# Attention output of a hybrid attention and RWKV-7 block: split values stationary, split exponentials moving, sums on GpSimd

## Chip, core and metric

The kernel runs on one core of one Trainium2 chip. The metric is device microseconds of one execution, lower is better; the median of three runs of the kernel before is 4223.68 us.

## What is computed

One layer of a diffusion block over 2048 latent tokens of width 1024 with a context prefix of 256 tokens. The part that the change touches is the banded attention: each of the 8 query heads (64 wide, 4 heads to a key and value head) reads the keys at most 128 tokens away, all 256 context keys and one sink, in one softmax.

```python
def latent_window_attention(q, k, v, kc, vc, sink):
    ...
    s_loc = jnp.einsum('bnqgrd,bnkgd->bngrqk', qb, kb).astype(jnp.float32) * scale
    s_ctx = jnp.einsum('bnqgrd,bcgd->bngrqc', qb, kc).astype(jnp.float32) * scale
    ...
    s_loc = jnp.where(valid[None, :, None, None], s_loc, -jnp.inf)
    ...
    p = jax.nn.softmax(jnp.concatenate([s_loc, s_ctx, s_sink], axis=-1), axis=-1)
    ...
    o = (jnp.einsum('bngrqk,bnkgd->bnqgrd', p_loc, vb)
         + jnp.einsum('bngrqc,bcgd->bnqgrd', p_ctx, vc))
    return o.reshape(B, L, N_Q_HEADS * dh)

def trunk_layer(x, xc, c, c_ctx, ...):
    ...
    ya = latent_window_attention(q, k, v, kc, vc, sink)
    ... # yr: bidirectional RWKV-7 scan, 64 wide heads, from the context's final state
    x = x + gate1 * merge_branches(ya, yr, gl, w_branch_attn, w_branch_rwkv, w_out)
    x = x + gate2 * sq_relu_mlp(modulate(rmsnorm(x, norm2_g), shift2, scale2), w_mlp_up, w_mlp_down)
```

## The kernel before

It runs in four stages. Until about 1100 us it normalises, projects and prepares the RWKV operands (`project`, `prepare`). From about 1100 to 2400 us the RWKV recurrence runs in 36 steps of 64 tokens and both directions, with the attention and a filler of gate and branch matrix products beside it. Then come merge and output projection, and from about 2750 us the MLP. The change lies in the second stage, apart from the line in `project` that stores the values.

**The recurrence.** A step goes through `chain_g` (TensorE, then a ScalarE copy of `g`), `chain_u` (TensorE, then ScalarE copies into `w`), `chain_s` (TensorE, then VectorE's product with `pc`), `turn` and `before` for the next step (TensorE into `gb`, then VectorE into `kr` and `bm`). Every four steps `inverse` inverts 32 by 32 triangles on VectorE: 31 pairs of small operations on `itmp` and `tn` (lines 588 and 590, each with two inputs in SBUF) and block transposes (lines 582, 599, 603).

**The attention.** There are 16 blocks of 128 queries. `scores(n)` loads the queries and (every second block) the keys, multiplies them head by head into `sc`, lets VectorE take minima of the rows, and writes the maximum as extra rows into `qB`. `outputs(n-1)` runs beside it: for each of 2 key heads `g` and each of 4 or 5 key blocks `b` (156 pairs in all) TensorE makes the transposed scores `sT`, 128 keys by 4 heads times 128 queries; ScalarE takes the exponential into `pT` (two buffers); and for each of the 4 heads a float32 product with `pT` as the stationary and `vtok` as the moving operand adds to `ops`. `vtok` holds 64 value columns and a column of ones, so column 64 of `ops` is the sum of the exponentials. VectorE adds the sink's term, takes the reciprocal and scales; TensorE transposes the result (`ot`), ScalarE copies it out, and it goes to `ya_d`.

**Order.** `attend` alternates steps of `scores` and `outputs`; `beside` runs one round of it, and one step of the filler `fill`, in every one of the six parts of a recurrence step. From this program order a scheduler sets each engine's order, and all engines run in order. `sc`, `sT`, `mt` and `ot` share two PSUM banks (`atp`), `ops` has one. All transfers go through SyncE's queue. A product of two operands that are split into two float32r parts is written as three float32r products (`gemm`, line 234).

## Time and profile before

| | us |
|---|---|
| runs (three), lowest, median, highest | 4222.08, 4223.68, 4229.45 |
| profiled execution | 4228.56 |
| its span, first to last instruction | 4226.8 |
| busy in the span: TensorE | 3865.3 (91%) |
| VectorE, ScalarE, GpSimd | 2171.9 (51%), 1359.5 (32%), 1349.6 (32%) |

Shares over the whole span mix stages with different limits: of GpSimd's 1349.6 busy us only 106.0 lie between 1130 and 2400 us, where the attention runs. So that stretch, from the first recurrence step to the last, is read by itself.

### The profile page before, as it was taken

To read this page: it belongs to the slowest core of one execution; us is meant where nothing else is said; L and a number is where in the kernel's file an instruction comes from. 1 tells how busy PE (TensorE), PEld (TensorE's weight loads), DVE (VectorE), ACT (ScalarE), POOL (GpSimd) and SP (SyncE) were. 2 spreads that over 40 slices of the span, in tenths; PEclk is the share of its full clock that TensorE was granted. 3 is DMA by queue.
4 is the path that set the end of the run, shared out by engine and by line. 5 is a ranking of instruction groups with operands and counts; after the bars stand their busy time and mean duration, and the time that the engine had idled before them with its cause. 6 is when DMAs were issued, how large, how long until landed. Compare 5 with 4: busy or idle time off the path is not lost.

```text
span 4226.8 us, 67796 instructions
## 1 busy us (share of the span) xinstructions
PE 3865.3 (91%) x26788; PEld 3148.4 (74%) x26788; DVE 2171.9 (51%) x3794; ACT 1359.5 (32%) x2476; POOL 1349.6 (32%) x1104
## 2 busy tenths in 40 slices
...
GB/s 236 202 195 158 161 183 188 188 185 184 164 138 138 125 131 148 106 132 96 131 139 83 158 150 179 176 154 65 70 50 40 60 41 130 69 60 60 40 55 45
DMA packets 617587, 529.95 MB, mean 125 GB/s; under 512 B 156212, under 2 KB 536340, under 8 KB 616244
## 3 DMA queue, kind: packets, MB, share of 16 engines
...
HBM read 381.09 MB, written 144.38 MB: 124 GB/s over the span
## 4 chain that ended last, share of the span: by engine, by line
PE 58%; DVE 6%; DMA 4%; issue 2%; POOL 2%; SPq 1%; ACT 1%; POOLq 0%; DVEq 0%; ACTq 0%
PE fd L1343 5%; PE fd L1344 5%; PE fd L1345 5%; PE fu L235 5%; PE fu L236 5%; PE fu L237 5%; PE ch L535 5%; PE gt L947 3%; PE ops L883 3%; PE gb L535 2%; DVE au L582 1%; PE sc L835 1%; PE mm L1260 1%; PE mm L1258 1%; PE mm L1259 1%
## 5 line engine op out<-in xcount | busy, mean ns | idle before, releaser
L235 PE MATMUL acc<-hh,w_hi 128*128 128x384 f32 (+6 forms) x1304 | 457.4, 353 | 41.6 <-ACT hh L211 18.9
L237 PE MATMUL acc<-hh,w_lo 128*128 128x384 f32 (+6 forms) x1304 | 455.8, 351 | 10.3 <-POOL w_lo L229 10.3
L236 PE MATMUL acc<-hl,w_hi 128*128 128x384 f32 (+6 forms) x1304 | 456.5, 351 | 4.8 <-POOL hl L212 4.8
L1349 DVE TENSOR_TENSOR acc<-fd,acc 128x512 f32<-128x512 f32 x480 | 322.3, 686 | 249.1 <-PE fd L1345 246.8
L235 PE MATMUL fu<-h2h,up_h 128*128 128x512 f32 x1024 | 403.4, 394 | 5.8 <-ACT rl L1330 5.8
L1343 PE MATMUL fd<-dn_h,g_h 128*128 128x512 f32 x1024 | 399.8, 390 | 3.5 <-DVE acc L1347 3.5
L236 PE MATMUL fu<-h2l,up_h 128*128 128x512 f32 x1024 | 402.6, 393 | 0.0
L237 PE MATMUL fu<-h2h,up_l 128*128 128x512 f32 x1024 | 402.0, 393 | 0.0
L1333 DVE TENSOR_TENSOR g_l<-rl,g_h 128x512 fp32r<-128x512 f32 x128 | 150.0, 1173 | 487.4 <-POOL rl L1332 487.4
L1344 PE MATMUL fd<-dn_l,g_h 128*128 128x512 f32 x1024 | 399.7, 390 | 0.0
L1345 PE MATMUL fd<-dn_h,g_l 128*128 128x512 f32 x1024 | 398.3, 390 | 0.0
L235 PEld LDWEIGHTS acc<-hh,w_hi 128*128 128x128 f32 (+2 forms) x1304 | 256.1, 197 | 67.1 <-ACT hh L211 21.8
L1332 POOL TENSOR_TENSOR rl<-rl 128x512 f32<-128x512 f32 x128 | 149.9, 1171 | 469.2 <-ACT g_h L1331 469.1
L229 POOL TENSOR_TENSOR w_lo<-w_raw,w_hi 128x1024 fp32r<-128x1024 f32 (+1 forms) x92 | 232.7, 2532 | 205.9 <-ACT w_hi L228 185.7
L1330 ACT ACTIVATE rl<-fu 128x512 f32<-128x512 f32 x128 | 76.2, 597 | 654.1 <-PE fu L237 644.9
L237 PEld LDWEIGHTS acc<-hh,w_lo 128*128 128x128 f32 (+2 forms) x1304 | 255.7, 196 | 31.4 <-POOL w_lo L229 12.5
L236 PEld LDWEIGHTS acc<-hl,w_hi 128*128 128x128 f32 (+2 forms) x1304 | 256.0, 196 | 25.1 <-POOL hl L212 6.0
L1287 POOL TENSOR_TENSOR dn_l<-raw,dn_h 128x1024 fp32r<-128x1024 f32 x64 | 155.6, 2450 | 275.1 <-ACT dn_h L1286 275.1
L845 DVE TENSOR_REDUCE mm<-sc 128x1 f32<-128x256 f32 (+1 forms) x256 | 119.0, 477 | 237.9 <-PE sc L837 152.2
L235 PEld LDWEIGHTS fu<-h2h,up_h 128*128 128x128 f32 x1024 | 193.1, 189 | 49.3 <-ACT rl L1330 6.0
L1343 PEld LDWEIGHTS fd<-dn_h,g_h 128*128 128x128 f32 x1024 | 192.9, 188 | 44.9 <-DVE acc L1347 4.0
L237 PEld LDWEIGHTS fu<-h2h,up_l 128*128 128x128 f32 x1024 | 192.7, 188 | 43.5
...
## 6 DMA issues: line engine op xcount, KB each, us to landing
...
```

The source lines that it names most:

```text
L229: pool.tensor_tensor(out=lo[:, :, :m], in0=raw[:, :, :m], in1=hi[:, :, :m].bitcast(F32), op=ALU.subtract)
L235: pe.matmul(ps[:m, :n], wh[:, k, :m], hh[:, k, :], start=(k == 0), stop=False)
L236: pe.matmul(ps[:m, :n], wh[:, k, :m], hl[:, k, :], start=False, stop=False)
L237: pe.matmul(ps[:m, :n], wl[:, k, :m], hh[:, k, :], start=False, stop=(k == KC - 1))
L535: return self.link(nc.tensor.matmul(*a, **k))
L1287: eng.tensor_tensor(out=lo, in0=raw, in1=hi.bitcast(F32), op=ALU.subtract)
L1332: pool.tensor_tensor(out=rl, in0=rl, in1=rl, op=ALU.mult)
L1333: dve.tensor_tensor(out=glo[:, j], in0=rl, in1=gh[:, j].bitcast(F32), op=ALU.subtract)
L1343: pe.matmul(ps, lh, dn[j][0][:, cs], start=(j == 0), stop=False)
L1344: pe.matmul(ps, lh, dn[j][1][:, cs], start=False, stop=False)
L1345: pe.matmul(ps, ll, dn[j][0][:, cs], start=False, stop=(j == FG - 1))
L1349: dve.tensor_tensor(out=acc[:, cs], in0=ps, in1=acc[:, cs], op=ALU.add)
```

## The change

The values are no longer kept in SBUF. `project` copies each transposed value tile once and stores it in `va_d`; `load_v` fetches a block of 128 tokens when the attention first needs it and splits it into a float32r part and a remainder, for head `g` side by side in 128 columns (in swapped order for the other head). In `outputs` the exponentials `pf` are split the same way: ScalarE copies them to `ph`, GpSimd subtracts into `pl`. Two float32r products, with the split values stationary and 512 moving columns (4 heads times 128 queries), replace the four float32 products; the output is then already transposed, with the two parts of the values in the two halves of the partitions, and VectorE adds the halves after a ScalarE copy. GpSimd adds the exponentials over the key blocks into `ts`; VectorE adds the sink's term into 8 partitions of `ts`; a float32 product with a matrix of ones sums over the partitions and broadcasts (`bc`), and VectorE takes the reciprocal of 128 by 512 elements and multiplies. `pT`, `ph` and `pl` have one buffer each. Keys are loaded for every block (384 tokens) rather than every second one (512), through the buffer `qraw` that queries and modulation weights use too.

```diff
@@ project
-                    for j in range(2):
-                        act.activation(vtok[:, t0 // P:t0 // P + n // P, j, 0:C],
-                                       tp[:, :n].rearrange("p (a b) -> p a b", b=P)[:, :, j * C:(j + 1) * C], AF.Copy)
+                    vt = epool.tile([P, 512], F32, name="st", bufs=3)
+                    act.activation(vt[:, :n], tp[:, :n], AF.Copy)
+                    sp.dma_start(out=va_d[t0 // P:(t0 + n) // P].rearrange("a p c -> p a c"),
+                                 in_=vt[:, :n].rearrange("p (a c) -> p a c", c=P))
...
+    def load_v(b):
+
+        raw = ap_.tile([P, 2, C], F32, name="vraw", bufs=1)
+        sp.dma_start(out=raw.rearrange("p g c -> p (g c)"), in_=va_d[b])
+        v = ap_.tile([P, 2, 2, C], F32R, name=f"vc{b}" if b < CTX // P else "vl", bufs=1 if b < CTX // P else 3)
+        for g in range(2):
+
+            act.activation(v[:, g, g], raw[:, g], AF.Copy)
+            dve.tensor_tensor(out=v[:, g, 1 - g], in0=raw[:, g], in1=v[:, g, g].bitcast(F32), op=ALU.subtract)
+        return v
...
+        raw = ap_.tile([P, 2, 512], F32, name="kraw", tag="qraw", bufs=1)
         for g in range(2):
-            raw = ap_.tile([P, 512], F32, name="kraw", tag="pT", bufs=2)
...
+        if n + 1 < NB:
+            load_kl(n + 1)
...
@@ outputs
-                pT = ap_.tile([P, NP, P], F32, name="pT", bufs=2)
-                act.activation(pT, sT, AF.Exp, scale=-1.0)
+                pf = ap_.tile([P, NP, P], F32, name="pT", bufs=1)
+                act.activation(pf, sT, AF.Exp, scale=-1.0)
+                ph = ap_.tile([P, NP, P], F32R, name="ph", bufs=1)
+                act.activation(ph, pf, AF.Copy)
+                pl = ap_.tile([P, NP, P], F32R, name="pl", bufs=1)
+                if b == 0:
+                    pool.tensor_copy(ts, pf)
+                else:
+                    pool.tensor_tensor(out=ts, in0=ts, in1=pf, op=ALU.add)
+                pool.tensor_tensor(out=pl, in0=pf, in1=ph.bitcast(F32), op=ALU.subtract)
                 yield
-                for a in range(NP):
-                    pe.matmul(op[:, a], pT[:, a], vtok[:, vb, g], start=(b == 0 and a == 0), stop=(b == nblk - 1),
-                              skip_group_check=True)
+                vg = v[:, g].rearrange("p a c -> p (a c)")
+                pe.matmul(op, vg, ph, start=(b == 0), stop=False)
+                pe.matmul(op, vg, pl, start=False, stop=(b == nblk - 1))
                 if b < nblk - 1:
                     yield
-            den = ap_.tile([P, 2, NP], F32, name="den", bufs=2)
-            dve.tensor_tensor(out=den[:, 0], in0=op[:, :, C], in1=k.es[:, g * NP:(g + 1) * NP], op=ALU.add)
-            dve.reciprocal(out=den[:, 1], in_=den[:, 0])
-            dve.tensor_tensor(out=on[:, :, g], in0=op[:, :, 0:C], in1=den[:, 1].unsqueeze(2).broadcast_to([P, NP, C]),
-                              op=ALU.mult)
+
+            r = hh[g]
+            act.activation(ob[r], op[hh[1 - g]].rearrange("p (a q) -> p a q", a=NP), AF.Copy)
+            dve.tensor_tensor(out=ob[r], in0=op[r].rearrange("p (a q) -> p a q", a=NP), in1=ob[r], op=ALU.add)
+            dve.scalar_tensor_tensor(out=ts[0:H], in0=k.tmp[0:H], scalar=cc[0:H, C_KS + g:C_KS + g + 1], in1=ts[0:H],
+                                     op0=ALU.mult, op1=ALU.add)
             yield
-        yield
-        ot = bank(atp, "ot", "at").rearrange("p (a q) -> p a q", a=NP)
-        for a in range(NP):
-            pe.transpose(ot[:, a], on[:, a].rearrange("p g c -> p (g c)"), ident)
-        ob = ap_.tile([P, NP, P], F32, name="ob", tag="atmp", bufs=1)
-        act.activation(ob, ot, AF.Copy)
+        bc = bank(atp, "bc", "at")
+        for g in range(2):
+            pe.matmul(bc[hh[g]], ones, sums[g], start=True, stop=True, skip_group_check=True)
+        bs = ap_.tile([P, NP, P], F32, name="ts", bufs=2)
+        dve.reciprocal(out=bs, in_=bc.rearrange("p (a q) -> p a q", a=NP))
+        dve.tensor_tensor(out=ob, in0=ob, in1=bs, op=ALU.mult)
         sp.dma_start(out=ya_d[:, :, n * P:(n + 1) * P].rearrange("a p t -> p a t"), in_=ob)
```

The order in which the engines find these instructions, at a block's end in recurrence step 20. In the names the number tells buffers apart; `ch0` and `ch1` are the recurrence's two directions, `tb` its transposes, and the number behind x counts repeats.

TensorE before: the last products into `ops`, then the transposes `ot`.

```order
L883 MATMUL ops_16133<-vtok_86,pT_16323 128x65 x4
L853 MATMUL mt_16447<-ident_76,pack_15826 72x128
L883 MATMUL ops_16133<-vtok_86,pT_16369 128x65 x4
L535 MATMUL ch1_16275<-g_16284,st_14853 64x64 x8
L535 MATMUL ch0_16264<-w_15851,ident_76 64x256 x2
L896 MATMUL ot_16484<-ident_76,on_15777 128x128 x4
L873 MATMUL sT_16648<-qA_15778,kAc_9615 128x512
L875 MATMUL sT_16648<-qB1_9628,kBc_9616 128x512
```

TensorE after the change, the same step.

```order
L920 MATMUL bc_16531<-ts_15745,ones_9614 64x512
L535 MATMUL ch0_16264<-bm_16124,w_15756 64x64 x8
L907 MATMUL ops_16180<-ph_16478,vl_15715 128x512
L535 MATMUL ch1_16275<-bm_16192,w_15767 64x64 x8
L535 MATMUL ch0_16264<-kr_15757,w_15756 64x64 x8
L535 MATMUL ch1_16275<-kr_15768,w_15767 64x64 x8
L538 MATMUL tb_16483<-ident_77,bks_16244 128x128 x4
L538 MATMUL tb_16490<-ident_77,bks_16255 128x128 x4
L908 MATMUL ops_16180<-pl_16480,vl_15715 128x512
L920 MATMUL bc_16531<-ts_16181,ones_9614 64x512
L889 MATMUL sT_16622<-qA_15721,kAc_9619 128x512
L891 MATMUL sT_16622<-qB1_9632,kBc_9620 128x512
```

The two products of one key block stand apart, with work of the recurrence between them, and the products with ones surround them; the next block's `sT` follows at once.

VectorE before, at the same block's end: the three operations that divide, among the inverse.

```order
L588 TENSOR_TENSOR itmp_15903<-tn_15816,au_15815 128x220
L888 TENSOR_TENSOR den_16443<-ops_16133,es_14869 128x4
L590 TENSOR_TENSOR tn_15816<-tn_15816,itmp_15903 128x22x10
L889 RECIPROCAL den_16443<-den_16443 128x4
L860 TENSOR_TENSOR qB1_9628<-atmp_16449,qB1_9628 8x512
L588 TENSOR_TENSOR itmp_15903<-tn_15816,au_15815 128x207
L890 TENSOR_TENSOR on_15777<-ops_16133,den_16443 128x4x64
```

VectorE after the change.

```order
L588 TENSOR_TENSOR itmp_16294<-tn_16208,au_16207 128x240
L922 RECIPROCAL ts_16534<-bc_16531 128x512
L590 TENSOR_TENSOR tn_16208<-tn_16208,itmp_16294 128x12x20
L914 TENSOR_TENSOR ob_15720<-ops_16180,ob_15720 64x512
L676 TENSOR_TENSOR kr_16243<-gb_16539,cc_84 64x256
L678 TENSOR_TENSOR bm_16538<-gb_16539,cc_84 128x256
L676 TENSOR_TENSOR kr_16243<-gb_16540,cc_84 64x256
L678 TENSOR_TENSOR bm_16538<-gb_16540,cc_84 128x256
L851 TENSOR_REDUCE mm_16694<-sc0_16695 128x1
L588 TENSOR_TENSOR itmp_16294<-tn_16208,au_16207 128x247
L851 TENSOR_REDUCE mm_16694<-sc1_16696 128x1
L923 TENSOR_TENSOR ob_15720<-ob_15720,ts_16534 128x512
```

The long reciprocal now stands ahead of the recurrence's `kr` and `bm` and of the minima that free the `sc` banks.

ScalarE before, some steps on, where a recurrence step begins (`g`, then `w`).

```order
L880 ACTIVATE pT_17097<-sT_17094 128x512
L880 ACTIVATE pT_17140<-sT_17137 128x512
L687 ACTIVATE g_17173<-ch0_17164 128x256
L687 ACTIVATE g_17184<-ch1_17175 128x256
L880 ACTIVATE pT_17229<-sT_17225 128x512
L694 ACTIVATE w_16653<-ch0_17164 64x256
L695 ACTIVATE w_16653<-ch0_17164 64x256
L694 ACTIVATE w_16664<-ch1_17175 64x256
L695 ACTIVATE w_16664<-ch1_17175 64x256
```

ScalarE after the change, at the beginning of a step.

```order
L896 ACTIVATE pT_16625<-sT_16622 128x512
L898 ACTIVATE ph_16627<-pT_16625 128x512
L687 ACTIVATE g_16663<-ch0_16654 128x256
L896 ACTIVATE pT_16714<-sT_16711 128x512
L898 ACTIVATE ph_16716<-pT_16714 128x512
L687 ACTIVATE g_16674<-ch1_16665 128x256
L694 ACTIVATE w_16242<-ch0_16654 64x256
L695 ACTIVATE w_16242<-ch0_16654 64x256
L896 ACTIVATE pT_16769<-sT_16765 128x512
L694 ACTIVATE w_16253<-ch1_16665 64x256
L695 ACTIVATE w_16253<-ch1_16665 64x256
L898 ACTIVATE ph_16771<-pT_16769 128x512
```

Each exponential is followed by its copy, and a second exponential, which writes the one `pT` buffer again, stands between the two `g` copies of the recurrence.

## Rows read from the trace of the kernel before

**Rows 1.** Busy us (count) by engine, granted clock, DMA share, GB/s: 1130 to 2400 us.
```profile
1130.00:2400.00 1270.00, 1140.92 (x13704) 896.45 (x13703) 714.78 (x1551) 415.06 (x796) 105.98 (x81) 0.90 0.44 126
```

**Rows 2.** Chain of waits, 1130 to 2400 us: its shares by line.
```profile
by line: PE ch L535 15.8%; PE ops L883 9.3%; PE gt L947 7.5%; PE gb L535 5.0%; DVE au L582 4.4%; issue 3.9%; PE sc L835 3.5%; PE sT L873 3.5%; DVE st L599 3.3%; PE sT L875 2.4%; PE sc L837 2.4%; PE g L535 2.2%; PE gt L988 1.9%; PE gt L989 1
```

**Rows 3.** Waits of TensorE, 1130 to 2400 us: total, times, longest.
```profile
PE sT L873 <- DVE mm L845: 26.3, 11, 5.9
PE sc L835 <- DVE qA L815: 11.9, 3, 6.1
PE ch L535 <- ACT w L695: 11.5, 8, 6.3
PE ch L535 <- DVE kr L676: 9.8, 3, 5.6
PE ch L535 <- DVE w L710: 9.6, 4, 8.3
```

**Rows 4.** Groups by line and form, TensorE: busy us, mean ns, idle before.
```profile
L883 PE MATMUL ops<-vtok,pT 128*128 128x65 f32 x1248 | 180.3, 291 | 3.9 <-ACT pT L880 3.7
...
L896 PE MATMUL ot<-ident,on 128*128 128x128 f32 x64 | 11.0, 298 | 8.5 <-DVE on L890 8.5
...
L1177 PE MATMUL mt<-sgt,g 96*128 96x512 f32 x32 | 20.9, 742 | 3.5 <-issue 2.6 <-ACT yw L1172 0.9
```

**Rows 5.** Timeline of TensorE, 1750 to 1772 us: start, duration.
```profile
1752.98 0.50 PE L873 MATMUL sT<-qA,kAl 128*128 128x512 f32 x1
1753.31 0.40 PE L875 MATMUL sT<-qB,kBl 128*128 128x512 f32 x1
1753.55 0.39 PE L878 MATMUL sT<-idb,amask 128*128 128x512 bf16 x1
...
1754.49 1.10 PE L883 MATMUL ops<-vtok,pT 128*128 128x65 f32 x8
1755.43 0.27 PE L853 MATMUL mt<-ident,pack 128*72 128x128 f32 x1
...
1767.45 1.92 PE L883 MATMUL ops<-vtok,pT 128*128 128x65 f32 x8
1769.13 0.56 PE L835 MATMUL sc<-kAc,qA 128*128 128x256 f32 x1
```

**Rows 6.** Groups by line and form, VectorE, 1100 to 2420 us.
```profile
L991 DVE SCALAR_TENSOR_TENSOR gt<-gt 128x512 f32<-128x512 f32 x32 | 21.9, 684 | 46.6 <-PE gt L990 26.9 <-DMA gt<-g_d 11.3 <-issue 4.4
...
L890 DVE TENSOR_TENSOR on<-ops,den 128x256 f32<-128x256 f32 x32 | 13.4, 420 | 0.6
...
L889 DVE RECIPROCAL den<-den 128x4 f32<-128x4 f32 x32 | 5.6, 174 | 0.7
...
L888 DVE TENSOR_TENSOR den<-ops,es 128x4 f32<-128x4 f32 x32 | 5.1, 160 | 19.5 <-PE ops L883 19.0
```

**Rows 7.** Line 590 in two stretches: VectorE busy us (count), clock, DMA.
```profile
1030.00:1500.00 470.00, 42.16 (x95) 0.95 0.50 139
1500.00:2400.00 900.00, 64.74 (x184) 0.87 0.42 123
```

**Rows 8.** Group by line and form, GpSimd, 1030 to 1500 us.
```profile
L929 POOL TENSOR_TENSOR gw_lo<-gw_raw,gw_hi 128x1024 fp32r<-128x1024 f32 x30 | 72.0, 2400 | 297.1 <-ACT gw_hi L928 242.9 <-PE gt L947 39.0 <-DMA kr<-ka_d 15.1
```

**Rows 9.** Groups by form, ScalarE and GpSimd, 1100 to 2420 us.
```profile
L880 ACT ACTIVATE pT<-sT 128x512 f32<-128x512 f32 x156 | 93.0, 596 | 298.5 <-PE sT L875 189.8 <-PE sT L878 107.4 <-DVE kBl L788 0.7
...
L898 ACT ACTIVATE ob<-ot 128x512 f32<-128x512 f32 x16 | 9.6, 597 | 11.2 <-PE ot L896 8.9 <-DVE qB L860 1.9 <-DVE bm L678 0.2
...
L978 ACT ACTIVATE ya_h<-raw 128x512 fp32r<-128x512 f32 x16 | 10.0, 628 | 27.6 <-DMA raw<-ya_d 27.5
...
L979 POOL TENSOR_TENSOR ya_l<-raw,ya_h 128x512 fp32r<-128x512 f32 x16 | 20.4, 1290 | 264.6 <-ACT ya_h L978 248.2 <-DMA raw<-ya_d 16.3
```

**Rows 10.** Waits of SyncE's queue, 1130 to 2400 us.
```profile
SPq L811 <- PE adp L117: 24.0, 7, 7.2
SPq L907 <- DVE qA L815: 23.0, 9, 4.5
```

77 lines of the change are left out of this document (41 added, 36 removed).

## Prediction

> **What bounds the kernel now.** I read the busy times by stretch first, since the change lies in one stage. Between 1130 and 2400 us TensorE is busy 1141 of 1270 us, VectorE 715, ScalarE 415 and GpSimd only 106, at a mean granted clock of 0.90 [rows 1]. So TensorE sets the pace, but it is idle 129 us. The chain of waits comes next: the products into `ops` hold 9.3% of it, 118 us, the recurrence's `ch` products most, and VectorE's block transposes (lines 582 and 599) 7.7% [rows 2]. Then TensorE's own waits: of the five longest, four end with VectorE, 26.3 + 11.9 + 9.8 + 9.6 = 57.6 us, and one with ScalarE, 11.5 us [rows 3]. The reader is to see two things: TensorE's work is worth nearly its whole time here, and the engine that makes TensorE wait is VectorE, to which this change gives work too. GpSimd ends none of the waits shown.
>
> **TensorE's work.** One key block of one head takes 8 records into `ops` (4 heads, two passes). At full clock they stand 0.94 us from start to the next instruction, at half clock 1.68 us; a pair of 512-column float32r products, as `sT` has it, takes 0.57 us [rows 5]. Busy time over all 156 is 180.3 us, 1.16 us each [rows 4]. The new pair is such a pair, for which I take 0.65 us with its share of half clock: 156 x (1.16 - 0.65) = 80 us saved. From below, the pair can cost 0.90 us by its records laid end to end (0.50 + 0.40), which leaves 40 us saved; from above 0.57 us, 92 us saved. The 64 transposes `ot` go, 11.0 us busy [rows 4], some 9 us without the overlap. New are 32 float32 products of 512 columns (`bc`). The nearest rows are the 16 products of line 1177, 2 records each, 20.9 us together, 1.31 us each: 42 us for 32, and half of that, 21 us, if the two halves, which fill different halves of the output, run beside one another [rows 4]. In the new order other rows stand between the two, so they mostly won't; I take 28 us since line 1177 runs partly at half clock. Sum: -80 - 9 + 28 = -61 us; bounds -82 and -7. What TensorE is given back reaches the end as far as TensorE is the bound, 1141 / 1270 = 0.9 [rows 1]: **-55 us**.
>
> **VectorE's work.** Gone are the sum, the reciprocal and the scaling: 13.4 + 5.6 + 5.1 = 24 us [rows 6]. New, per block: two additions of the halves (64 x 512) and two of the sink's term (8 x 512), each 0.68 us by line 991, the nearest 512-column row: 4 x 16 x 0.68 = 44 us; one product of 128 x 512, 11 us; key and value remainders, some 14 us at the same rate per element. The reciprocal now has 512 elements a partition instead of 4. Line 889 takes 174 ns, line 888 with the same 4 elements 160 [rows 6]; 14 ns over 4 elements are 3.5 ns an element beyond an ordinary operation. So it costs between 0.68 us, if those 14 ns are fixed, and 0.68 + 512 x 3.5 ns = 2.5 us; were the ordinary part of line 889 10 ns shorter than line 888, which reads PSUM, it would be 6 ns an element and 3.7 us. I take 2.5 us, these being the only rows with a reciprocal: 40 us over 16. Net +44 + 11 + 14 + 40 - 24 = **+85 us**, bounds +56 and +104. The Trainium skill (VectorE: DVE Perf Modes, section "First, the fixed hardware budget") says that reciprocal is an iterative divide with a repeat count of 8. If that were 8 cycles an element, my estimate from the page's clock would be about 4.3 us, and the sum would rise by 16 x 1.8 x 0.25 = 7 us; the 14 ns speak for something between.
>
> **VectorE against GpSimd.** GpSimd gets 32 copies, 124 additions and 156 subtractions of 128 x 512. An operation of this size takes 1.29 us [rows 9]; a copy has no row, I put it at 0.8, between 0.3 and 1.29. That is 280 x 1.29 + 32 x 0.8 = 387 us, where GpSimd was idle. It isn't free: line 590, two SBUF inputs on VectorE, takes 42.16 / 95 = 0.444 us between 1030 and 1500 us and 64.74 / 184 = 0.352 us after [rows 7], and in the first stretch GpSimd has 72 us of two-input work on `gw_lo` [rows 8]. The excess is 95 x 0.092 = 8.7 us, 0.12 us per us of GpSimd: 387 x 0.12 = 46 us on line 590 alone. Line 588, 815 and the new two-input operations meet the same; I take **65 us**, bounds 0 (if they miss one another) and 147 (the rival below).
>
> What 85 + 65 = 150 us more of VectorE cost: the shown waits are 57.6 us on 715 busy, 0.08 us per us. With VectorE at 68% instead of 56% of the stage a further us meets TensorE waiting more often. I take 0.25, between 0.08 and 0.5: **+38 us**, bounds +5 and +115. At a block's end it is concrete: the reciprocal stands ahead of `kr`, `bm` and the minima; behind it wait the recurrence's next `chain_g` and the `sc` products, since `bc` holds one of the two shared banks until the reciprocal has read it. The wait of `ot` for `on`, 8.5 us [rows 4], only changes into that of `bc` for `ts`.
>
> **ScalarE.** 156 copies `ph` at 0.63 us are 98 us, 32 half evacuations at 0.6 are 19, `ob` goes (-10) [rows 9], key and value splits add some 12: +119 us. The shown waits for ScalarE are 11.5 on 415 us, 0.03 per us [rows 1, 3]; I take 0.05, **+6 us**, bounds 0 and +25. Behind the copies queue the `g` and `w` copies of the recurrence.
>
> **The new wait.** The remainder `pl` is ready after the exponential (0.60 us) and two GpSimd operations (2.58 us) [rows 9], 3.2 us after `sT`, where `pT` was ready after 0.6. Between them stand rows of the recurrence and the scores, as the order at the block's end shows, and they cover most of it. With one buffer each the next exponential also waits for GpSimd's subtraction, and the recurrence's second `g` copy waits behind it. Nothing in the trace shows this wait. From below it is 0; from above 156 x 0.85 us = 133 us if each key block sees 2.35 us of cover. One block lasts about 70 us for 10 key blocks, 7 us each, twice what the path needs, so I take **+20 us**.
>
> **SyncE.** 32 more key and 18 value loads, and keys now share the one buffer for which the queue already waits 24.0 and 23.0 us [rows 10]: **+4 us**, bounds 0 and +25. The six stores of `va_d` lie in the first stage, where values are not needed for hundreds of us: nothing. The new order also ends the attention two recurrence steps earlier, which moves filler and costs nothing by the busy share.
>
> **Sum.** -55 + 38 + 6 + 20 + 4 = +13 us. The profiled execution took 4228.6 us, so it becomes 4241.6; the median of the runs is 4.9 us lower, 4223.7, and the forecast is **4237 us**.
>
> **Rivals.**
> 1. *TensorE's saving arrives.* VectorE's extra work falls into its 44% idle time, and the path through GpSimd is covered everywhere: -55 + 85 x 0.08 + 3 = -45, **4179 us**; at the upper bounds 4223.7 - 82 x 0.9 + 10 = 4160. For it speaks that TensorE is the bound [rows 1] and that GpSimd was idle; against it that VectorE ends most of the waits [rows 3]. It decides if VectorE's waits stay near 80 us.
> 2. *Gain and cost cancel*, within 0.2% (8.4 us, about what a measurement of this kernel can tell from no change): **4224 us**. That is the forecast with 13 us less, a third off VectorE's factor.
> 3. *GpSimd and VectorE exclude each other for whole instructions.* Then about 500 operations of the inverse and 160 others find GpSimd busy for 387 of 1270 us plus its old share, 35%, and wait half an operation: 660 x 0.35 x 0.64 = 147 us instead of 65, +82 x 0.25 = +20, **4257 us**. Line 590's 0.12 speaks for less. The Trainium skill (SBUF — State Buffer, section "SBUF: two separate sides") states such a lock, held for a whole instruction, for VectorE operations with two SBUF inputs against GpSimd ones; that the line 590 rows grow only beside GpSimd work agrees with its direction.
> 4. *The path is not covered.* TensorE runs in order and stands at each `pl` product: +133 instead of +20, **4350 us**, slower. It decides from the point where the rows between `sT` and the `pl` product take less than 3.2 us at most key blocks. For it speaks the single buffer; against it the 7 us per key block.
> 5. *The pair is not cheaper*: 0.90 us, so -7 us of TensorE instead of -61. That would give 4286 and is in the forecast's range.
>
> **Chances.** Forecast 0.31 (its own range 4233 to 4300), rival 1 0.34, rival 2 0.17, rival 3 0.08, rival 4 0.10. Faster by over 0.2% is rival 1: 0.34. Within 0.2%: 0.17. Slower: 0.31 + 0.08 + 0.10 = 0.49. The range leaves out most of rival 4 and a tenth of the faster cases: 4162 to 4325 us.
>
> **What would show it.** Right: between 1130 and the end of the stage TensorE's busy time falls by 50 to 70 us and its idle time grows by more, with VectorE's lines (`mm`, `kr`, `w`, the reciprocal) as releasers; line 922 near 2.5 us; lines 588 and 590 some 20% longer in the mean; GpSimd busy near 490 us. Wrong: TensorE's waits on VectorE unchanged (rival 1); waits of `ops` on `pl` above 60 us (rival 4); a granted clock that moves by more than 0.03 in the stage, on which I count nothing.

## The result and the profile after

The changed kernel takes **4336.3 us** (median of 4 runs, 4328.1 to 4344.8) against 4226.6 us of the kernel before beside it. The ratio is 1.0256, 95% interval 1.0227 to 1.0285: by the ratio some 108 us slower, where 13 us slower was forecast and the range ended at 4325. The profiled execution has a span of 4331.7 us at a mean granted clock of 0.923 (before 4226.8 and 0.932).

The page after: part 1 (busy time, share of the span, instructions), and of part 4 the chain that ended last, by engine; below it the same shares before.

```profile
PE 3881.4 (90%) x25852; PEld 3085.9 (71%) x25852; DVE 2391.2 (55%) x3843; ACT 1472.9 (34%) x2694; POOL 1732.2 (40%) x1416
...
PE 49%; DVE 14%; DMA 5%; issue 2%; POOL 2%; ACT 1%; SPq 1%; POOLq 0%; DVEq 0%; ACTq 0%
```

```profile
PE 58%; DVE 6%; DMA 4%; issue 2%; POOL 2%; SPq 1%; ACT 1%; POOLq 0%; DVEq 0%; ACTq 0%
```

Of the span's chain VectorE now holds 14% instead of 6%, TensorE 49% instead of 58%. TensorE is no busier than before (3881 against 3865 us); VectorE has 219 us more, and GpSimd 383 us.

The stage of the change after, with the columns of [rows 1] (busy us and count of TensorE, its weight loads, VectorE, ScalarE and GpSimd, then granted clock, DMA share, GB/s).

```profile
1130.00:2400.00 1270.00, 1076.45 (x11564) 767.94 (x11564) 883.93 (x1533) 504.96 (x962) 489.58 (x389) 0.88 0.42 118
```

TensorE's busy time fell from 1141 to 1076 us. That isn't work saved: only 11564 matmul records lie in the stretch, where before 13704 did, of which the change itself takes away 936 (26788 on the page before, 25852 after). The stage has become longer, so that the stretch holds less of the program, and TensorE idles 194 us in the stretch instead of 129. VectorE rose from 715 to 884 us, and the granted clock fell from 0.90 to 0.88.

The chain of waits over the same stretch, after (answers to [rows 2]).

```profile
by line: PE ch L535 9.4%; DVE itmp L588 8.0%; DVE tn L590 7.4%; issue 5.6%; PE gt L972 5.1%; DVE au L582 4.1%; DVE st L599 4.0%; DVE mm L851 2.7%; PE g L535 2.3%; PE gb L535 2.2%; DVE ts L922 2.2%; PE sc L841 2.2%; PE sT L889 2.2%; DVE kr L
```

The products into `ops`, 9.3% of it before, are gone from the shares shown. In their place stand two lines of the inverse, 588 and 590, with 8.0% and 7.4%: together 196 us, where before neither was among the shares shown. The reciprocal (line 922) has 2.2%, 28 us.

TensorE's waits in the stretch, after (answers to [rows 3]; total us, times, longest).

```profile
PE sT L889 <- DVE mm L851: 53.4, 23, 6.8
PE ch L535 <- DVE w L710: 20.4, 17, 4.0
PE gb L535 <- issue: 13.8, 5, 5.7
PE sc L841 <- DVE ts L922: 11.4, 6, 3.1
PE sc L841 <- DVE mm L851: 10.6, 8, 2.5
PE ch L535 <- DVE kr L676: 10.4, 4, 3.7
...
PE ops L908 <- POOL pl L904: 5.5, 6, 1.4
```

The wait of `sT` for the minima doubled, from 26.3 to 53.4 us, and that for `w` too, from 9.6 to 20.4. The new wait, `ops` for `pl`, is 5.5 us: for TensorE GpSimd's path is short enough. GpSimd hardly ever makes TensorE wait directly. Two other waits for its results are longer: line 915 on VectorE waits 18.3 us for the sum (in the fence of VectorE's groups below), and ScalarE's exponential 18.1 us for the subtraction that still reads the one `pT` buffer (line 896 for line 904, 1130 to 2500 us).

Groups by form after, TensorE's products of the new part (answers to [rows 4]).

```profile
L908 PE MATMUL ops<-pl,vl 128*128 128x512 f32 x92 | 45.0, 489 | 3.7 <-POOL pl L904 3.6
...
L907 PE MATMUL ops<-ph,vl 128*128 128x512 f32 x92 | 43.8, 476 | 0.7 <-ACT ph L898 0.6
...
L920 PE MATMUL bc<-ts,ones 128*64 128x512 f32 x64 | 37.7, 685 | 10.0 <-DVE ts L915 6.2 <-ACT pT L896 2.9 <-DVE atmp L861 0.8
```

Groups by form after, VectorE: the reciprocal, the two additions at a block's end, and one narrow form of line 588 (answers to [rows 6]); the same form in the kernel before stands in the fence below it.

```profile
L922 DVE RECIPROCAL ts<-bc 128x512 f32<-128x512 f32 x16 | 53.7, 3354 | 5.4 <-PE bc L920 5.2
L915 DVE SCALAR_TENSOR_TENSOR ts<-atmp,cc,ts 8x512 f32<-8x512 f32 x32 | 34.7, 1086 | 18.7 <-POOL ts L903 18.3
...
L914 DVE TENSOR_TENSOR ob<-ops,ob 64x512 f32<-64x512 f32 x32 | 21.9, 686 | 10.0 <-ACT ob L913 9.5
...
L588 DVE TENSOR_TENSOR itmp<-tn,au 128x60 f32<-128x60 f32 x16 | 11.9, 742 | 0.3
...
L923 DVE TENSOR_TENSOR ob<-ob,ts 128x512 f32<-128x512 f32 x16 | 11.6, 728 | 0.1
```

```profile
L588 DVE TENSOR_TENSOR itmp<-tn,au 128x60 f32<-128x60 f32 x16 | 4.4, 277 | 0.3
```

The same instruction, 60 columns of two SBUF inputs, takes 742 ns in the mean instead of 277. Nothing in it has changed. It is one of the most lengthened; with 112 columns the same line stands at 275 ns, before at 273. Line 915, 8 partitions of `ts`, takes 1086 ns, where a 512-column row had 684 [rows 6].

Groups by form after, GpSimd: the sum and the remainder, and the first block's copy (answers to [rows 9]).

```profile
L904 POOL TENSOR_TENSOR pl<-pT,ph 128x512 fp32r<-128x512 f32 x156 | 210.1, 1347 | 74.8 <-ACT ph L898 37.5 <-PE ops L908 29.1 <-DVE ada_rows L938 3.9
L903 POOL TENSOR_TENSOR ts<-ts,pT 128x512 f32<-128x512 f32 x124 | 161.2, 1300 | 434.9 <-ACT pT L896 418.3 <-PE sc L848 8.6 <-PE gt L972 4.6
...
L901 POOL COPY ts<-pT 128x512 f32<-128x512 f32 x32 | 21.4, 670 | 137.6 <-ACT pT L896 135.0 <-PE bc L920 2.6
```

312 operations, 393 us, as counted (387). Most of the idle time before them ends with ScalarE: GpSimd is not overloaded.

What happens there is plain in one moment, after: start, duration, engine and line, first VectorE, then GpSimd, then TensorE.

```profile
1760.15 0.25 DVE L588 TENSOR_TENSOR itmp<-tn,au 128x87 f32<-128x87 f32 x1
1760.43 1.21 DVE L590 TENSOR_TENSOR tn<-tn,itmp 128x87 f32<-128x87 f32 x1
1761.68 1.19 DVE L588 TENSOR_TENSOR itmp<-tn,au 128x60 f32<-128x60 f32 x1
1762.90 0.22 DVE L590 TENSOR_TENSOR tn<-tn,itmp 128x60 f32<-128x60 f32 x1
...
1764.42 3.83 DVE L599 STREAM_TRANSPOSE st<-tn 32x1024 f32<-32x1024 f32 x2
```

```profile
1760.23 1.31 POOL L903 TENSOR_TENSOR ts<-ts,pT 128x512 f32<-128x512 f32 x1 [4.55 <-ACT pT L896]
1761.50 1.28 POOL L904 TENSOR_TENSOR pl<-pT,ph 128x512 fp32r<-128x512 f32 x1
```

```profile
1764.61 0.46 PE L535 MATMUL gb<-kr,bks 64*128 64x128 f32 x2 [2.64 <-issue]
...
1769.16 2.04 PE L535 MATMUL gb<-kr,bks 64*128 64x128 f32 x14 [3.38 <-DVE bm L678]
```

Line 588 with 87 columns takes 0.25 us; it starts at 1760.15, just before GpSimd's addition (1760.23). Line 590 with the same 87 columns starts at 1760.43, 0.2 us after a GpSimd addition, and ends at 1761.64, when that addition ends (1761.54): 1.21 us. The next, 60 columns, starts 0.18 us after GpSimd's subtraction and ends with it too: 1.19 us. When GpSimd is through, 60 columns take 0.22 us. Behind the inverse queue `kr`, `bm` and the transpose, and TensorE stands idle for 2.64 us and then 3.38 us, the second of them put down to `bm`. That shows how the loss arises: nobody waits for GpSimd's result here, but VectorE's instructions last until GpSimd's end. It is only a part of these two gaps, some 1.9 us by the four rows of VectorE; the two transposes, 3.83 us, belong to the inverse in both kernels.

One moment could be picked; a count over the trace between 1130 and 2500 us cannot. Of the 496 operations of lines 588 and 590, 350 meet no GpSimd instruction and take 335 ns in the mean, 426 at most; 144 meet one that reads SBUF and take 987 ns. Of the 110 that start while such an instruction runs, 108 end within 0.3 us of its end.

The Trainium skill (SBUF — State Buffer, section "SBUF: two separate sides") states this as an exclusive lock, held for a whole instruction, between a VectorE operation with two SBUF inputs and a GpSimd operation that reads SBUF. These rows agree with it, and the run e1_memset below with its condition that GpSimd reads (184 us on the two lines there, 260 here).

### The profile page after: what moved, and what is told of

It reads as the page before. It is cut to its first block, busy times and chain, and to the rows that moved or that the text cites. A ratio compares the mean times of both kernels' runs of the same rounds, so it can differ in the third digit from the quotient of the medians.

```text
span 4331.7 us, 66828 instructions
## 1 busy us (share of the span) xinstructions
PE 3881.4 (90%) x25852; PEld 3085.9 (71%) x25852; DVE 2391.2 (55%) x3843; ACT 1472.9 (34%) x2694; POOL 1732.2 (40%) x1416
## 4 chain that ended last, share of the span: by engine, by line
PE 49%; DVE 14%; DMA 5%; issue 2%; POOL 2%; ACT 1%; SPq 1%; POOLq 0%; DVEq 0%; ACTq 0%
PE fu L234 5%; PE fd L1371 5%; PE fd L1372 5%; PE fu L235 5%; PE fu L236 5%; PE fd L1373 5%; PE ch L535 3%; DVE itmp L588 2%; DVE tn L590 2%; PE gt L972 1%; DVE st L599 1%; DVE au L582 1%; PE mm L1286 1%; PE mm L1287 1%; PE mm L1288 1%
## 5 line engine op out<-in xcount | busy, mean ns | idle before, releaser
L1361 DVE TENSOR_TENSOR g_l<-rl,g_h 128x512 fp32r<-128x512 f32 x128 | 163.2, 1276 | 485.3 <-POOL rl L1360 485.3
L903 POOL TENSOR_TENSOR ts<-ts,pT 128x512 f32<-128x512 f32 x124 | 161.2, 1300 | 434.9 <-ACT pT L896 418.3
L904 POOL TENSOR_TENSOR pl<-pT,ph 128x512 fp32r<-128x512 f32 x156 | 210.1, 1347 | 74.8 <-ACT ph L898 37.5
```

The source lines that it names most:

```text
L903: pool.tensor_tensor(out=ts, in0=ts, in1=pf, op=ALU.add)
L904: pool.tensor_tensor(out=pl, in0=pf, in1=ph.bitcast(F32), op=ALU.subtract)
L1361: dve.tensor_tensor(out=glo[:, j], in0=rl, in1=gh[:, j].bitcast(F32), op=ALU.subtract)
```

## The experiments

Times are medians, ratios go against the kernel before in the same series of runs, with 95% intervals. "588 + 590" is the busy time of these two lines between 1130 and 2500 us, 496 instructions in every kernel; "VectorE" is its busy time over the whole program. The forecast is put in the places that each run tells apart: theory A is that VectorE and GpSimd exclude one another and that this lengthens the inverse; the rivals are the reciprocal and VectorE's other work at a block's end (theory B), the pair of products and the longer path to it (theory C), and a TensorE saving that was there and was hidden. The kernel before took 4211 to 4227 us in the median of these series. For each kernel the scheduler orders the engines anew, so a run can differ from its neighbour in more than its edit; where that was found, it is said.

| run | what it is | time, us | ratio | interval | 588 + 590 | VectorE |
|---|---|---|---|---|---|---|
| after | the change | 4336 | 1.0256 | 1.0227 to 1.0285 | 260 | 2391 |
| e1_memset | after, GpSimd writes only | 4245 | 1.0074 | 1.0052 to 1.0096 | 184 | 2285 |
| e2_norecip | after, reciprocal a copy | 4318 | 1.0250 | 1.0229 to 1.0271 | 266 | 2335 |
| e3_nosum | after, no sum on GpSimd | 4289 | 1.0151 | 1.0134 to 1.0168 | 227 | 2331 |
| e12_halves | after, GpSimd in halves | 4315 | 1.0202 | 1.0176 to 1.0229 | 241 | 2357 |
| e5_no_split | after, no remainder, no sum | 4225 | 1.0029 | 1.0015 to 1.0043 | 186 | 2289 |
| e6_pe_only | e5 without reciprocal and sink | 4218 | 1.0004 | 0.9986 to 1.0023 | 182 | 2219 |
| before | | 4211 to 4227 | 1 | | 177 | 2172 |
| e4_before_pool | before + 2 GpSimd additions | 4234 | 1.0047 | 1.0031 to 1.0063 | 224 | 2234 |
| e8_before_pool4 | before + 4 GpSimd additions | 4317 | 1.0247 | 1.0218 to 1.0276 | 288 | 2308 |
| e9_before_dve | before + VectorE minimum | 4224 | 1.0025 | 1.0004 to 1.0046 | 183 | 2267 |
| e10_before_both | before + both | 4264 | 1.0119 | 1.0087 to 1.0151 | 221 | 2320 |
| e11_before_bf16pv | before, `ops` products in bf16 | 4167 | 0.9851 | 0.9830 to 0.9872 | 189 | 2191 |
| e13_before_pe | before + `sT` twice | 4232 | 1.0021 | 1.0008 to 1.0035 | 181 | 2188 |
| e14_bf16pv_pe | e11 + `sT` twice | 4176 | 0.9904 | 0.9876 to 0.9931 | 186 | 2187 |
| e15_after_pe | after + `sT` twice | 4362 | 1.0347 | 1.0321 to 1.0374 | 261 | 2400 |

**e1_memset: GpSimd as busy, but reading nothing.** Sum and remainder are left out; `ts`, `pT` and `pl` are set instead.

```diff
                 if b == 0:
-                    pool.tensor_copy(ts, pf)
+                    pool.memset(ts, 1.0)
                 else:
-                    pool.tensor_tensor(out=ts, in0=ts, in1=pf, op=ALU.add)
-                pool.tensor_tensor(out=pl, in0=pf, in1=ph.bitcast(F32), op=ALU.subtract)
+                    for _ in range(2):
+                        pool.memset(pf, 0.0)
+                for _ in range(3):
+                    pool.memset(pl.bitcast(F32), 0.0)
```

> The changed kernel, with GpSimd's sum and subtraction replaced by memsets of about the same total length on the same tiles (the sums of the exponentials and the remainder product are left out): GpSimd stays as busy but reads nothing. Theory A (VectorE operations with two SBUF inputs and GpSimd operations that read SBUF exclude each other, and this lengthening of VectorE's lines is the main cause): lines 588 and 590 go from 260 back to about 180 us of VectorE, and the time falls by 60 to 90 us, to about 4255 us. Theory B (the work that VectorE was given at a block's end, the reciprocal first, is the main cause): the time stays within 15 us of 4336. Theory C (the pair of products and the longer path to them are no gain for TensorE): also within 15 us of 4336.

Of the change's 2.56% it leaves 0.74%: 1.82%, 77 us, are given back. The two lines of the inverse stand at 184 us, near the 177 of the kernel before. Busy time of line 588, then of line 590, between 1130 and 2500 us, in the changed kernel and in this one (columns as in [rows 7]).

```profile
1130.00:2500.00 1370.00, 132.75 (x248) 0.88 0.42 119
```

```profile
1130.00:2500.00 1370.00, 127.31 (x248) 0.88 0.42 119
```

```profile
1130.00:2500.00 1370.00, 93.73 (x248) 0.89 0.44 128
```

```profile
1130.00:2500.00 1370.00, 90.23 (x248) 0.89 0.44 128
```

GpSimd is busy 530 us in that stretch, more than the 495 us of the changed kernel. Counted within this run, 208 operations of the two lines meet only memsets and take 345 ns in the mean, 427 at most; 261 meet nothing and take 331 ns; the 27 that meet a GpSimd instruction that reads take 960 ns. So it is GpSimd's reading that lengthens the inverse, and not that it is busy.

The 77 us are not the reading's alone, though. Without the sum, line 915 no longer waits for it (2.4 us instead of 18.3). And the order of this kernel is another: the two products of a key block follow one another directly in 108 of the 156 cases, in the changed kernel in 43, and TensorE is busy 153 us on `ops` and `bc` instead of 187. If that wait cost its whole 16 us, and TensorE's 34 us a half each (the highest price found below), these two would be 33 us, and 44 of the 77 would be left for the lengthening. That is an estimate from these rows; no run separates the three. The chain in the stage shows the two lines fall back.

```profile
by line: PE ch L535 11.2%; PE gt L974 6.8%; issue 6.2%; DVE st L599 3.8%; DVE itmp L588 3.5%; DVE au L582 3.5%; DVE tn L590 3.5%; PE gb L535 2.9%; PE sT L889 2.8%; PE g L535 2.4%; PE ops L909 2.3%; DVE mm L851 2.3%; PE sc L841 2.2%; PE gt L
```

**e2_norecip: is it the reciprocal?** The reciprocal becomes a copy; the division is left out.

```diff
-        dve.reciprocal(out=bs, in_=bc.rearrange("p (a q) -> p a q", a=NP))
+        dve.tensor_copy(bs, bc.rearrange("p (a q) -> p a q", a=NP))
```

> The changed kernel with the reciprocal of 128 x 512 (3.35 us, 16 times) replaced by a copy of the same shape (0.69 us): the division is left out, 43 us of VectorE gone, and the shared bank is free 2.7 us earlier. Theory B: 40 to 60 us less, about 4285 us. Theory A: 10 to 20 us less, about 4320. Theory C: within 10 us of 4336.

1.0250 against 1.0256: no difference that these runs can tell, although VectorE has 56 us less. The rival falls. In the changed kernel TensorE's waits put down to line 922 are 17 us (11.4 for `sc`, 5.4 for `sT`) of the 54 us that the line is busy; without the reciprocal they do not come back as time.

**e5_no_split and e6_pe_only: what is left without GpSimd.** In e5 the exponential is written once, as float32r, in two buffers; both products take it, GpSimd sets `ts` once and does nothing else (remainder and sum are left out). e6 also makes the reciprocal a copy and leaves the sink's term out.

```diff
-                pf = ap_.tile([P, NP, P], F32, name="pT", bufs=1)
-                act.activation(pf, sT, AF.Exp, scale=-1.0)
-                ph = ap_.tile([P, NP, P], F32R, name="ph", bufs=1)
-                act.activation(ph, pf, AF.Copy)
-                pl = ap_.tile([P, NP, P], F32R, name="pl", bufs=1)
+                ph = ap_.tile([P, NP, P], F32R, name="ph", bufs=2)
+                act.activation(ph, sT, AF.Exp, scale=-1.0)
...
-                pe.matmul(op, vg, pl, start=False, stop=(b == nblk - 1))
+                pe.matmul(op, vg, ph, start=False, stop=(b == nblk - 1))
```

e6 on top of it:

```diff
-            dve.scalar_tensor_tensor(out=ts[0:H], in0=k.tmp[0:H], scalar=cc[0:H, C_KS + g:C_KS + g + 1], in1=ts[0:H],
-                                     op0=ALU.mult, op1=ALU.add)
...
-        dve.reciprocal(out=bs, in_=bc.rearrange("p (a q) -> p a q", a=NP))
+        dve.tensor_copy(bs, bc.rearrange("p (a q) -> p a q", a=NP))
```

> The changed kernel without GpSimd's part: the exponential is written as float32r at once (two buffers), both products take it, the sum is a tile of ones (remainder and sum left out; TensorE's work and the reciprocal stay). It shows what the pair of products alone is worth with the extra VectorE work of a block's end. Theory A: 90 to 120 us less than the changed kernel, about 4225 us, since the TensorE saving of some 30 us is eaten by the reciprocal. Theory B: 30 us less, about 4305. Theory C: 50 us less at most, about 4290.

> The changed kernel without GpSimd's part and without the two VectorE items at a block's end: both products take the copied exponentials as they are, GpSimd sums nothing, the reciprocal is a copy and the sink's term is not added (remainder, sum, sink and division are left out). What is left is the pair of products, the product with ones, the half additions and the key and value splits. Theory A (TensorE's saving is small: the busy time into `ops` fell by 31 us only, and the product with ones gives most of it back) expects 4205 to 4225 us, at most 0.4% below the kernel before. Rival (the saving is there, and VectorE's new work at a block's end hides it) expects 4160 to 4185 us.

e6 is level with the kernel before (1.0004). Its pair of products is cheaper, as the fence shows: 46.6 + 38.6 + 31.4 + 26.5 = 143 us by groups, 117 us without the overlap, against 180 us before. `bc` takes 18.9 us, since its two halves follow one another here, and the transposes' 11 us are gone: 56 us less for TensorE in all, and nothing for the program. The rival of a hidden saving falls as theory A had it: with GpSimd's part and VectorE's items at a block's end gone, it does not appear.

```profile
L901 PE MATMUL ops<-ph,vl 128*128 128x512 f32 x92 | 46.6, 506 | 7.1 <-ACT ph L896 7.1
...
L902 PE MATMUL ops<-ph,vl 128*128 128x512 f32 x92 | 38.6, 419 | 0.0
...
L901 PE MATMUL ops<-ph,vc 128*128 128x512 f32 x64 | 31.4, 490 | 8.3 <-ACT ph L896 4.7 <-DVE ob L908 3.6
...
L902 PE MATMUL ops<-ph,vc 128*128 128x512 f32 x64 | 26.5, 413 | 0.0
...
L912 PE MATMUL bc<-ts,ones 128*64 128x512 f32 x64 | 18.9, 672 | 0.0
```

With e1 these runs split the loss into steps: e5 is at 0.29% (12 us), which is the pair with `bc`, the splits and the block's end; from e5 to e1 it is 0.45% (19 us), ScalarE's copies, the path through GpSimd and the single buffers; from e1 to the changed kernel 1.82% (77 us), GpSimd's reading above all. Sum 108 us. The steps are not pure: TensorE is busy 136 us on `ops` and `bc` in e5, where the two products of a key block follow one another in 152 of 156 cases, 153 us in e1 and 187 us in the changed kernel. So 51 us of TensorE's work that the changed kernel's order costs lie in the two later steps.

**e4_before_pool and e8_before_pool4: the same lengthening in the kernel before.** Two, then four GpSimd additions of the exponentials per key block, result unused (in both the mask's identity is kept once instead of four times, to make room).

```diff
                 act.activation(pT, sT, AF.Exp, scale=-1.0)
+                for _ in range(4):
+                    jk = ap_.tile([P, NP, P], BF16, name="jk", bufs=1)
+                    pool.tensor_tensor(out=jk, in0=pT, in1=pT, op=ALU.add)
```

> The kernel before, with two GpSimd additions of 128 x 512 per key block that read pT twice and write a tile that nobody reads (bfloat16, for space; the identity for the mask is broadcast instead of stored four times). Nothing else of the change. Theory A: lines 588 and 590 grow from 177 to 240 us or more, and the time by 40 to 80 us, to about 4285 us. Theories B and C: within 12 us of the kernel before.

> The kernel before with four GpSimd additions of the exponentials (128 by 512, result unused) for each key block, 624 in all, some 650 us, twice what gave +20 us. If the price is linear in GpSimd's time: +40 us, ratio 1.010, and lines 588 and 590 some 95 us longer in the stage. If it is convex (VectorE's idle time absorbs the first part only): +70 to +110 us, ratio 1.017 to 1.026.

330 us of GpSimd lengthen the two lines by 47 us and cost 20 us, less than theory A had written down (63 us or more, and 40 to 80 us); 667 us lengthen them by 111 us and cost 104 us. The price is convex: the first 62 us on VectorE cost 0.3 for each us, the next 74 us 84 us, 1.1 each. Not all of that need come through VectorE: with four additions ScalarE's exponential waits 16.7 us for an addition that still reads its `pT` buffer, with two 1.8 us. No run separates the two. The chain of the stage in e8 shows the same two lines rise to near where the changed kernel has them.

```profile
by line: PE ch L535 10.0%; DVE itmp L588 7.1%; PE ops L885 6.8%; DVE tn L590 6.6%; PE gt L949 6.0%; issue 5.9%; PE gb L535 4.6%; DVE st L599 3.6%; DVE au L582 3.3%; PE sc L834 2.7%; PE sT L872 2.7%; PE g L535 2.1%; PE sc L836 1.9%; PE sT L8
```

So a cost of the change's size can be had without the change: four GpSimd additions for each key block make the kernel before as slow.

**e9_before_dve and e10_before_both: VectorE's own work, alone and with GpSimd.**

```diff
                 act.activation(pT, sT, AF.Exp, scale=-1.0)
+                dj = ap_.tile([P, NP], F32, name="dj", bufs=2)
+                dve.tensor_reduce(out=dj, in_=pT, axis=AX.X, op=ALU.min)
```

> The kernel before with one more VectorE operation for each key block: a minimum over the 512 exponentials, result unused, 156 x some 0.57 us = 90 us, about what the changed kernel gives VectorE besides the lengthened inverse. GpSimd gets nothing. Theory A (VectorE's own work is cheap by itself) expects +10 to +25 us, 0.1 to 0.3 us for each us; the rival (VectorE's own work costs near its whole time) +60 to +90 us.

> The kernel before with both: two GpSimd additions (325 us) and the VectorE minimum (90 us) for each key block. If the two prices only add, this is the sum of the two runs with one each, about +20 for GpSimd and what the VectorE run gives, some 35 to 45 us. If the price of a lengthened VectorE operation grows with VectorE's load, it is clearly more: 60 to 100 us.

95 us more on VectorE cost 10 us, 0.11 each. With GpSimd's two additions on top, 53 us more on VectorE cost a further 40 us, 0.75 each; here too ScalarE's exponentials wait for the additions, 13.8 us. The sum of the single prices would be 0.72%, measured is 1.19% with an interval that begins at 0.87%: more than additive, though less than the 60 to 100 us written down for a growing price, and by little more than the intervals allow.

**e3_nosum and e12_halves: less of it, and smaller pieces.** e3 leaves the sum out (`ts` is set to one, the denominators are left out) and keeps the subtraction; e12 cuts each GpSimd operation into two of 256 columns.

```diff
-                    pool.tensor_copy(ts, pf)
-                else:
-                    pool.tensor_tensor(out=ts, in0=ts, in1=pf, op=ALU.add)
+                    pool.memset(ts, 1.0)
```

```diff
-                    pool.tensor_tensor(out=ts, in0=ts, in1=pf, op=ALU.add)
-                pool.tensor_tensor(out=pl, in0=pf, in1=ph.bitcast(F32), op=ALU.subtract)
+                for a in (0, 2):
...
+                        pool.tensor_tensor(out=ts[:, a:a + 2], in0=ts[:, a:a + 2], in1=pf[:, a:a + 2], op=ALU.add)
+                for a in (0, 2):
+                    pool.tensor_tensor(out=pl[:, a:a + 2], in0=pf[:, a:a + 2], in1=ph[:, a:a + 2].bitcast(F32), op=ALU.subtract)
```

> The changed kernel without GpSimd's sum of the exponentials (the denominators are left out; each `ts` is set to one): 156 subtractions of 1.3 us are left of the 312 operations, about what 'the kernel before with two additions' has in time but on the fuller VectorE. Lines 588 and 590: some 220 us, between 186 without GpSimd and 260. If the price is convex in GpSimd's time: 55 to 90 us less than the changed kernel, 4240 to 4270 us. If it is linear: 35 to 50 us less, 4275 to 4290 us.

> The changed kernel with each of GpSimd's operations on the exponentials cut into two of 256 columns: the same elements, twice the instructions (560), each some 0.7 us instead of 1.3. If VectorE waits for the whole GpSimd instruction, each hit costs half: lines 588 and 590 fall from 260 us to some 220 in the stage, and the time by 20 to 50 us. If the two share the port by elements, 588 and 590 stay within 10 us and the time does not fall.

e3 gives back 1.05%, 44 us, as the linear expectation had it. That fits a curve whose cheap part the changed kernel has used up, but does not show it, since e3 also takes away line 915's wait for the sum (0.6 us instead of 18.3) and half of TensorE's time on `bc` (19 us instead of 38). e12 gives back 0.54%, some 23 us (with both intervals, 6 to 39), although GpSimd itself takes 454 us instead of 393. The two lines fall by 19 us, half of what was expected. That the pieces' size counts speaks for waiting until an instruction ends; that more GpSimd time lengthens VectorE less speaks against sharing by elements. e12 moves little else: TensorE has 185 us on `ops` and `bc` instead of 187, line 915 waits 11.1 us instead of 18.3, and ScalarE's exponentials wait for GpSimd even longer, 37.6 us instead of 18.1.

From these pairs the price of a VectorE microsecond can be laid side by side:

| pair | VectorE, us more | time, us more | each |
|---|---|---|---|
| e9 over before: own work | 95 | 10 | 0.11 |
| e5 over e6: reciprocal, sink | 70 | 11 | 0.15 |
| after over e2: reciprocal | 56 | 3 | 0.05 |
| e4 over before: lengthened by GpSimd | 62 | 20 | 0.32 |
| e3 over e1: lengthened by GpSimd | 45 | 32 | 0.72 |
| e12 over e1: lengthened by GpSimd | 72 | 54 | 0.75 |
| e10 over e9: lengthened by GpSimd | 53 | 40 | 0.75 |
| after over e12: lengthened by GpSimd | 34 | 23 | 0.7 |
| after over e1: lengthened by GpSimd | 106 | 77 | 0.73 |
| e8 over e4: lengthened by GpSimd | 74 | 84 | 1.1 |

Single rows are uncertain by 10 to 20 us of time, and some hold more than VectorE: those over e1 line 915's wait and TensorE's order, those of e8 and e10 ScalarE's waits. They are upper readings of the price. But the two kinds stand apart: added work 0.05 to 0.15, operations that GpSimd lengthens about 0.7 (76 of the 106 us of the changed kernel are lines 588 and 590), with e4, the first and smallest dose in the kernel before, between them.

**e11_before_bf16pv and e13_before_pe: what a TensorE microsecond is worth.** e11 keeps exponentials and values in bf16, so `ops` takes one pass, at bf16's precision; e13 does the pair into `sT` twice.

```diff
-    vtok = keep.tile([P, T // P, 2, C + 1], F32, name="vtok")
+    vtok = keep.tile([P, T // P, 2, C + 1], BF16, name="vtok")
...
-                pT = ap_.tile([P, NP, P], F32, name="pT", bufs=2)
+                pT = ap_.tile([P, NP, P], BF16, name="pT", bufs=2)
```

```diff
                 pe.matmul(sT, kA[:, g, k0:k0 + P], qA[:, g], start=True, stop=False)
+                pe.matmul(sT, kB[:, g, k0:k0 + P], qB[:, g], start=False, stop=True)
+                pe.matmul(sT, kA[:, g, k0:k0 + P], qA[:, g], start=True, stop=False)
```

> The kernel before with exponentials and values in bf16, so that the products into `ops` take one pass instead of two (precision is given up, nothing else moves). Their busy time should fall from 180 us to some 60 to 90. If a TensorE microsecond is worth 0.9 at the end, as the prediction took it: 80 to 110 us less, ratio 0.974 to 0.981. Theory A (in this stage TensorE's relief mostly turns into waiting for VectorE and the recurrence): 0 to 35 us less.

> The kernel before with the pair of products into `sT` done twice for each key block: 156 pairs, some 90 us more work for TensorE, nothing else. At 0.9 for each us: +80 us, ratio 1.019. If a TensorE microsecond is worth 0.1 to 0.4 here: +10 to +35 us.

The busy time into `ops` fell from 180 to 47 us, 133 us less, and the time by 1.49%, 63 us: 0.47 for each. e13 adds 74 us of busy time on `sT` and costs 0.21%, 9 us: 0.1 for each. Both lie under 0.9, and they differ; e11 lies between its two expectations, e13 just under the lower one. The granted clock may be one reason. Busy us by engine, clock, DMA share and GB/s of two stretches, in the kernel before, in e11 and in e13.

```profile
1450.00:1750.00 300.00, 272.72 (x3380) 216.62 (x3378) 167.91 (x368) 103.05 (x203) 26.59 (x22) 0.90 0.44 129
1750.00:2050.00 300.00, 258.64 (x3289) 203.88 (x3290) 177.18 (x386) 90.49 (x177) 9.43 (x12) 0.85 0.41 117
```

```profile
1450.00:1750.00 300.00, 251.54 (x3391) 190.14 (x3391) 184.64 (x392) 107.12 (x214) 20.50 (x20) 0.87 0.46 133
1750.00:2050.00 300.00, 241.67 (x3234) 181.92 (x3235) 200.18 (x437) 97.58 (x189) 15.06 (x16) 0.85 0.45 130
```

```profile
1450.00:1750.00 300.00, 278.99 (x3377) 220.42 (x3375) 169.40 (x363) 105.32 (x202) 31.80 (x26) 0.96 0.46 133
1750.00:2050.00 300.00, 268.61 (x3449) 209.54 (x3447) 178.49 (x391) 94.78 (x188) 9.53 (x12) 0.94 0.43 123
```

With more to do TensorE was granted 0.96 and 0.94 of its full clock instead of 0.90 and 0.85, with less to do 0.87 and 0.85. The engine has two levels, 1.2 and 2.4 GHz, so 0.85 is a mean: 30% of the stretch at the lower one. By and large the clock stands higher in these rows where TensorE is busier (not in every pair: 0.85 at 258.64 us, 0.87 at 251.54). That would take back part of what shorter work gives, and pay for part of what longer work costs; these rows do not show that it does.

**e14_bf16pv_pe and e15_after_pe: does the clock explain it?** The same doubled `sT` in e11 and in the changed kernel.

> The kernel before with the bf16 products into `ops` (133 us less work, which gave 63 us) and the pair into `sT` done twice (some 90 us more). If the falling clock ate half of the gain, the added products bring the clock back from 0.87 and cost little: 4160 to 4180 us. If a TensorE microsecond is worth what the bf16 run showed, 0.47: +42 us, 4205 to 4215 us.

> The changed kernel with the pair of products into `sT` done twice for each key block, some 90 us more work for TensorE. In the kernel before this cost +9 us, while the granted clock between 1450 and 2050 us stood at 0.94 to 0.96 instead of 0.85 to 0.90. If the clock that falls when TensorE waits is part of the change's loss, the same thing happens here: the clock of the stage rises from 0.88 to some 0.92, and the time stays within 15 us of the changed kernel's 4336. If the clock does not answer, TensorE's 90 us cost at least 0.5 for each us: 4375 to 4420 us.

The stage in e14 and in e15, columns as in [rows 1].

```profile
1130.00:2400.00 1270.00, 1094.73 (x13486) 829.03 (x13544) 735.14 (x1587) 423.86 (x809) 130.04 (x103) 0.92 0.45 132
```

```profile
1130.00:2400.00 1270.00, 1100.19 (x11704) 794.63 (x11705) 865.48 (x1484) 500.91 (x951) 478.32 (x383) 0.92 0.40 116
```

In both the clock of the stage rises as expected, from 0.88 to 0.92. The doubled pair costs 0.53% in e14, some 22 us (7 to 37 with both intervals). The trace of e14 holds only 625 of its 684 matmul records on `sT`, busy 191 us; by their mean all of them are an estimated 209 us, 72 more than in e11 (137): 0.3 each. The time lies where "the clock ate half" put it, but for 72 us the other theory, 0.47 each, gives 34 us, which the interval holds too, so e14 does not tell them apart. In e15 it costs 0.91%, 38 us for 76 us of busy time, 0.5 each, between its two expectations: the time pays although the clock rises, and the theory that the fallen clock is a part of the change's loss finds no support. So the granted clock is higher with the added work in all three kernels, and a microsecond of TensorE is worth 0.1 to 0.5 in four runs; how much of what is missing to 0.9 the clock takes, and how much the waits for VectorE, stays open.

## Why the prediction was wrong

The direction held, the size did not: +13 us was forecast, +108 us measured. Two steps make up most of the 95 us between them: the factor 0.25 on the lengthened inverse (28 to 61 us too little), and TensorE's -55 us, which did not come. By the terms of the sum:

- **"What TensorE is given back reaches the end as far as TensorE is the bound, 0.9": wrong.** It is 0.1 to 0.5 by e13, e14, e11 and e15, and nothing at all in e6, whose TensorE has 56 us less. Even at 0.47 those would be 26 us; e6's added work on VectorE (47 us at 0.11) takes 5 of them, and where the other 20 go was not found: the splits, the half additions and the key loads of every block are left in it. A busy share of 90% is not a price: it does not tell how much of that work would have stood beside a wait anyway.
- **-61 us of TensorE's work: mis-sized, below its lower bound.** Products into `ops` fell by 31 us, not 80. The two products stand apart in the new order in 113 of 156 cases (the rows of the order already showed one such case) and then don't overlap: 149 us over 156 pairs, 0.96 us each, where the rows laid end to end gave 0.90 and I took 0.65. Rival 5, "the pair is not cheaper", was nearer. In e6, where they follow one another, a pair takes 0.75 us. `bc` took 38 us instead of 28. In all -31 - 11 + 38 = -4 us, where the bound was -7.
- **+85 us of VectorE's own work: too low, and it hardly mattered.** e5 has 117 us more on VectorE than the kernel before, 12 us of them in a later stage. The reciprocal took 3.354 us, not 2.5, which is less than the 3.7 and 4.3 us of the two other readings; beyond an ordinary operation's 0.68 us that is 5.2 ns an element, between the 3.5 ns that I took from line 889 and the 6 ns that I named beside it. Its price is 0.05 to 0.15 for each us, under the 0.25 taken.
- **+65 us of lock: too low.** It was 106 us (VectorE of the changed kernel over e1), 76 us of it on the two lines, which became 47% longer, not 20%. I had scaled line 590's excess in a stretch where GpSimd worked on `gw_lo`, 0.12 us per us; it came to 0.27 (106 over 393). The direction and the mechanism were those of rival 3, whole instructions; its 147 us were too high. (By its own rule the share was (387 + 106) / 1270 = 39%, not 35%, and the time 164 us; and 0.5 times the upper bounds, 104 + 147, is 125 us, not the +115 given. Neither slip moves the forecast.)
- **The factor 0.25 for both: the step that failed most.** It treated VectorE's time as one thing. The lengthened inverse costs about 0.7 for each us (after over e12, with 0.73 over e1 as an upper reading), and lines 588 and 590 take one another's result, step after step, with the recurrence behind them. That is 77 us at most and 44 by the estimate under e1, where the sum had 65 x 0.25 = 16. Rival 3, with the right mechanism, carried the same factor and so came to 4257 only.
- **+20 us for the new wait and +6 us for ScalarE: together about right.** From e5 to e1 19 us are lost, which holds both, and 17 us more work for TensorE besides. As a wait of TensorE `pl` shows 5.5 us, and rival 4 is excluded; the path shows instead as ScalarE's wait of 18.1 us.
- **+4 us for SyncE** was not measured by itself; it may be part of the 20 us that are open in e6.
- **The granted clock**, on which I counted nothing, moved by 0.02, inside the 0.03 that I allowed. That it rises with added work (e13) is one candidate for what is missing to 0.9.

Of the signs named, VectorE's `mm`, `w` and the reciprocal did grow as releasers of TensorE's waits, and GpSimd was busy 490 us. TensorE's busy time in the stretch fell by 65 us as named, but by luck: the stretch holds less of the program, and the work that the change takes away was 4 us.

With the measured steps, which are differences between runs and not pure terms, the sum is: the pair with all its loads, splits and block ends +12, ScalarE and the path +19, the lock with what hangs on it +77.

A version faster than both is e11: the kernel before with exponentials and values in bf16, 4167 us, ratio 0.9851 (0.9830 to 0.9872). It pays with precision in the values and weights, keeps the sum of the exponentials on TensorE in a column of ones, and gives GpSimd nothing.
